# A hybrid attention block: scaling later, another order beside the search, another first attention block

## The chip, the cores and the metric

One core of one Trainium2 chip runs the whole layer in one launch. The metric is the device time of that launch in microseconds, the median of three runs. Most of the text speaks of engines by short names: PE does matmuls (TensorE), DVE is VectorE, ACT is ScalarE, POOL is GpSimd, and SP (SyncE) issues nearly all DMAs, in order.

## The reference

One layer over 2048 tokens of width 1024, in float32:

```python
xn = rms_norm(h, norm_gain)
qa, ka, va, ga, qb, kb, vb, gb, iq, ik, iw, za, zb = split(xn @ w_in)
ya = chunked_relpos_attention(qa, ka, va, rel_bias) * silu(ga)      # 8 heads, own chunk of 64 + 8 before it
yb = dsa_sparse_attention(rope(qb), rope(kb), vb, rope(iq), rope(ik), iw) * silu(gb)
merged = sigmoid(za + b0) * (ya @ w_branch_a) + sigmoid(zb + b1) * (yb @ w_branch_b)
out = rms_norm(h + merged @ w_out, final_norm_gain)
```

The sparse attention scores every admissible key with a small indexer, `score = sum_h relu(iq_h · ik) * iw_h`, keeps the 256 best keys of each query, and attends to those with one shared key and value head.

## The kernel before

**Numbers and tiles.** Every operand of a matmul is split into a high and a low part (names with `h` and `l`, or index 0 and 1), and a product is three matmuls (`mm3`, L210 to L218). ACT makes the high part (a copy to the fast format), DVE or POOL the low part (a subtraction). Tokens come in four groups g of 512. Two slots of transposed, normed x are held on chip (`xh`, `xl`; `SLOT[g]`); groups 0 and 1 use them first, groups 3 and 2 after a reload.

**Units and jobs.** The columns of `w_in` are 20 units: zb and za (four each), gb, ga, qb, va, ka, qa (two each). A standard job is one unit for one group: 2 accumulators of 24 matmuls with 512 columns, or, for the value units va, 4 accumulators of 24 matmuls with 288 columns. Weights come through `wst` (L204 to L209): ACT splits, POOL subtracts.

1. 0 to 100 us: norm, and the projection for the indexer.
2. 100 to 622 us: the first pass, all units for groups 0 and 1. Between its matmuls the indexer's logits are computed (L479 on PE, L481 on ACT, L486 on DVE) and the top-256 threshold of each row is searched: a first guess (L514 to L530), seven passes (L531 to L552, on ACT and DVE in turn), and a sweep (L553 to L569). This work is a set of threads; `tick` pumps them after each accumulator by an amount (`PUMP`, `PUMP2`) against costs that the threads yield. In jobs `EN0` to `EN0 + 15` (8 to 23), `load_early` brings x of groups 3 and 2 and `norm_early` scales it (ACT L1249, POOL L1250), stores it (`xnD`) and forms the block sums that stage 4 uses (`sumD`).
3. 622 to 787 us: the switch. `norm_again` returns queued closures that reload a slot from `xnD`, four for each group, popped from the list `again` during jobs. Then the left-over jobs for groups 3 and 2. When no thread is left, `close_search` adds up whether any row missed its tolerance, which PE does with a 1x1 matmul (L581, tile `bad`); this matmul stands in PE's order.
4. 787 to 1075 us: quads. A unit for groups 2 and 3 and both column halves at once, by Strassen's scheme: 7 products of 12 matmuls, 84 where 96 would stand. `QUADS` lists the 14 units that go so.
5. 1075 to about 1900 us: attention. The list `seq` orders units A(g, h) (a head of branch A for a group) and B(block, heads); `LEAD` units of A come first, then whichever branch is behind by the costs `cost`; `GB` is the order of the groups of B. Each unit's scores run one unit ahead of its outputs, its loads (`qz`, `kk`, `vs`, `qsB`) two ahead. After the last head or block of a group, `extra` places calls of `branch`: 128 columns of `y @ w_branch`, weights through `dst` and `dw`, gate `sig`, result `dt`; the first of the two branches to arrive stores it, the second adds it (`ta`).
6. To 2108 us: output projection (L1457) and the final norm.

**Pools.** Tiles come from pools that are opened at the left or the right end of the on-chip memory. A pool that lies where another lay waits for the last reader there. A tile asked for again in a ring of `bufs` copies waits for the last reader of the copy before.

Of the kernel before, what the change touches and what calls it, by code (L numbers as in the profile page):

```python
# [8 lines left out]
F32 = mybir.dt.float32  # L9
F32R = mybir.dt.float32r  # L10
# [36 lines left out]
WK, WAT = 5, 1  # L47
SPL, LEAD = 96, 3
GB, C0_ = (1, 0, 2, 3), 14
CA_, CB_, TAILB = 26, 9, 260  # L50
# [4 lines left out]
WE = False  # L55
QUADS = "za ka za gb za ka gb zb zb qb ga qa ga qa"
WSB, NB = 4, 5
# [25 lines left out]
def f32(ap):  # L83
    return ap.bitcast(F32)
# [11 lines left out]
def block_kernel(ctx: ExitStack, tc: tile.TileContext, io, dbg=None):  # L96
# [576 lines left out]

    def hl_tile(tag):
        if early_:
            return ev.tile([128, 512], F32R, name=tag + "t", tag="ef")
        return evl.tile([128, 512], F32R, name=tag, tag=tag)

    early_ = []

# [36 lines left out]
    def evac_v(c, g, o, acc):  # L717
        vv = ev.tile([128, 2, 32], F32R, name="vvt", tag="ef") if early_ else evl.tile([128, 2, 32], F32R, name="vv", tag="vv")
        nc.scalar.activation(vv[:, 0], acc[:, 256:288], AF.Copy)
        nc.vector.tensor_tensor(vv[:, 1], acc[:, 256:288], f32(vv[:, 0]), op=OP.subtract)  # L720
        nc.sync.dma_start(vB[:, 4 * g + o, :].rearrange("p (l c d) -> p c l d", l=2, c=2)[:, c], f32(vv))
        acc = acc[:, 0:256]
        e = hl_tile("eh").rearrange("p (h l d) -> p h l d", h=4, l=2)
        v = acc.rearrange("p (h d) -> p h d", h=4)
        nc.scalar.activation(e[:, :, 0, :], v, AF.Copy)
        nc.vector.tensor_tensor(e[:, :, 1, :], v, f32(e[:, :, 0, :]), op=OP.subtract)
        nc.sync.dma_start(vA[g][c * 4:c * 4 + 4, :, o, :].rearrange("h p n -> p h n"), f32(e).rearrange("p h l d -> p h (l d)"))
# [7 lines left out]
    nq = len(quads)  # L735
    rest = [u for k in ("qb", "zb", "za", "gb", "ga", "ka", "qa") for u in left[k]]
    jobs = [("std", u, u, g) for u in range(nu - 2) for g in (0, 1)]
    jobs += [("std", u, u, g) for g in (1, 0) for u in (a_, b_)]
    jobs += [("std", nu + u, u, g) for g in (3, 2) for u in va]
    jobs += [("std", nu + u, u, g) for u in rest for g in (3, 2)]  # L740
    turned = max(i for i, j_ in enumerate(jobs) if j_[3] == 3)
# [40 lines left out]
    def open_early():  # L782

        nonlocal sml, wk, wy, wz, dna, wp_, pe
        dna = dph.enter_context(pool("dna", side="right"))
        wp_ = dph.enter_context(pool("wp_", side="right"))
        sml = ph.enter_context(pool("sml", bufs=4, side="right"))
        wk = ph.enter_context(pool("wk", bufs=2, side="right"))
        wy = ph.enter_context(pool("wy", bufs=2, side="right"))
        wz = ph.enter_context(pool("wz", side="right"))  # L790
        pe = dph.enter_context(pool("pe", space=PSUM, side="right"))

    def open_late():
        nonlocal dn, att, ldb, wp2, pl_ps, psd, kBt, vBt, mk01
        late.append(1)
        dn = dph.enter_context(pool("dn", bufs=2))
        att = ph.enter_context(pool("att"))
# [293 lines left out]
    def branch(m, G, c):  # L1091
# [3 lines left out]
        nc.sync.dma_start(st, io["wA" if m == "a" else "wB"][c])  # L1095
        wt = dn.tile([128, 2, 4, 128], F32R, name="dw", tag="dw", bufs=1)
        nc.scalar.activation(wt[:, 0], st, AF.Copy)  # L1097
# [8 lines left out]
        if (G, c) not in half_done:  # L1106
            half_done.add((G, c))
            nc.sync.dma_start(tD[G, :, c, :], t_)
            return
        ta = dn.tile([128, 512], F32, name="ta", tag="ta")  # L1110
        nc.sync.dma_start(ta, tD[G, :, c, :])
# [61 lines left out]
    def load_m(t):  # L1173

        mts[t] = wp_.tile([128, 2, KT, 256], F32R, name="mm", tag=f"P{(t // 2) % 2}")
        g, o = divmod(t, 4)
        for k in range(0, KT, 2):
            mf = dn.tile([128, 2, 256], F32, name="mf", tag="ta")
            nc.sync.dma_start(mf, mD[g, :, k:k + 2, o * 128:o * 128 + 256])
            nc.scalar.activation(mts[t][:, 0, k:k + 2], mf, AF.Copy)  # L1180
            (nc.vector if t < 2 else nc.gpsimd).tensor_tensor(mts[t][:, 1, k:k + 2], mf, f32(mts[t][:, 0, k:k + 2]), op=OP.subtract)
# [51 lines left out]

    def load_early(g, k):

        xs = tkl.tile([128, 2, 512], F32, name="xs", tag="xs", bufs=2)
        nc.sync.dma_start(xs, io["xT"][g][:, k::4, :])
        xa = None
# [80 lines left out]
    for i, (how, r_, u, g) in enumerate(jobs):  # L1319
        kind, c2 = UNITS[u]  # L1320
        wt, s_ = wcur[r_], SLOT[g]
        rate[0] = PUMP2 if r_ >= nu and kind != "va" else PUMP[2 if i < SLOW else kind in DVE_KINDS]
        if EN0 <= i < EN0 + 16:
            (norm_early if i % 2 else load_early)(3 - (i - EN0) // 8, (i - EN0) // 2 % 4)
        for c in range(4 if kind == "va" else 2):
# [10 lines left out]
            else:  # L1336
# [4 lines left out]
                busy = bool(again) and not early_  # L1341
                for _ in range(1 if busy and len(again) < 3 else 2):
                    if again:
                        again.pop(0)()
# [22 lines left out]
    S2, S1, S4 = (of_sum(n) for n in ("s2", "s1", "s4"))  # L1367
    parts_ = {}

# [192 lines left out]
```

## Time and profile before

| what | value |
|---|---|
| median of 3 runs | 2110.87 us (2108.78 to 2114.64) |
| the profiled execution | 2109.7 us, its span 2107.9 us |
| granted clock of TensorE, mean | 0.986 |
| PE busy | 2006.3 us, 95% |
| DVE, ACT, POOL busy | 70%, 61%, 39% |
| DMA | 333.76 MB, mean 158 GB/s |

The span is the time from the first to the last instruction that the profiler recorded. PE is busy in almost all of it, so the places that matter are the few in which it is not; the windows in the prediction list them. In a row of waits, the numbers are us in total, times, and the longest; in a row of groups, busy us and mean ns, then the idle time ahead of them and what ended it; in a row of the timeline, start and length in us.

### The profile page before, as it was taken

The page shows a single profiled execution, that of the slowest core. Times are in us where ns is not written, and L with a number is a line of the kernel's source. Part 1 is how long each engine was busy: PE and PEld are TensorE (multiplying, and loading weights), DVE is VectorE, ACT ScalarE, POOL GpSimd, SP SyncE. Part 2 cuts the span into 40 slices and gives each one's busy share as a digit, 9 for nine tenths or more (in the row PEclk, how much of TensorE's full clock was granted, in tenths as well). Part 3 has the DMA queues.
Part 4 walks back from the last instruction along what each step waited for, and adds up shares of the span by engine and source line. Part 5 has one row for each costly group of instructions (what it writes and reads, how often), then busy time and mean ns, then how long its engine had stood idle before and what let it go on. Part 6 is the DMA issues. An engine that isn't in the chain of part 4 may idle for free.

```text
span 2107.9 us, 33647 instructions
## 1 busy us (share of the span) xinstructions
PE 2006.3 (95%) x10706; PEld 1693.5 (80%) x10706; DVE 1466.2 (70%) x3738; ACT 1285.3 (61%) x2644; POOL 813.7 (39%) x992
## 2 busy tenths in 40 slices
PE   8798999999998999999979999899999999999998
PEld 7576788889878877878757888788988888888786
DVE  6738888788879667556547676766876678775434
ACT  5465566756565645555449787866987678773221
POOL 2146212231232136545425544566444643434410
PEclk9899999999999999999989999999999999999999
DMA  9487433354564544343564646576345630335642
GB/s 359 145 283 258 151 110 113 110 193 141 171 201 133 176 141 133 109 130 115 165 181 138 191 139 186 174 220 210 111 138 158 187 118 21 101 101 195 203 137 90
DMA packets 225926, 333.76 MB, mean 158 GB/s; under 512 B 28624, under 2 KB 99664, under 8 KB 225616
## 3 DMA queue, kind: packets, MB, share of 16 engines
q1 hardware_dynamic: 225744, 331.57, 49.1%
q8 instruction: 85, 1.39, 0.3%
q14 instruction: 97, 0.79, 0.1%
HBM read 219.33 MB, written 112.16 MB: 157 GB/s over the span
## 4 chain that ended last, share of the span: by engine, by line
PE 62%; DMA 13%; DVE 9%; ACT 5%; POOL 5%; issue 4%; SPq 2%; POOLq 0%; DVEq 0%; ACTq 0%
PE acc L217 23%; PE d L217 6%; PE po L1457 6%; PE O L1053 5%; PE pt L1045 5%; PE s L1028 5%; DMA wst<-wS 4%; PE O L950 3%; PE s L906 2%; PE lg L479 2%; PE pt L940 2%; DMA dst<-wB 1%; PE xa L217 1%; DMA dst<-wA 1%; DVE P L832 1%
## 5 line engine op out<-in xcount | busy, mean ns | idle before, releaser
L217 PE MATMUL acc<-xh,wt 128*128 128x512 f32 x1856 | 605.4, 396 | 5.3 <-DVE e L337 3.3
L217 PEld LDWEIGHTS acc<-xh,wt 128*128 128x128 f32 x1856 | 349.9, 189 | 86.3 <-DVE e L337 3.5
L217 PE MATMUL acc<-xl,wt 128*128 128x512 f32 x928 | 365.9, 394 | 0.0
L209 POOL TENSOR_TENSOR wt<-wst,wt 128x512 fp32r<-128x512 f32 (+1 forms) x108 | 137.6, 1305 | 428.9 <-ACT wt L208 372.3
L853 POOL TENSOR_TENSOR ptl<-pf,pth 128x512 fp32r<-128x512 f32 (+1 forms) x144 | 180.5, 1253 | 227.1 <-ACT pf L849 148.6
L856 DVE TENSOR_TENSOR ptl<-pt,pth 128x512 fp32r<-128x512 f32 (+1 forms) x288 | 187.0, 658 | 46.1 <-ACT pth L855 44.7
L486 DVE SCALAR_TENSOR_TENSOR sc<-lg,iw,sc 128x512 f32<-128x512 f32 (+2 forms) x266 | 179.1, 679 | 52.9 <-ACT lg L481 47.0
L217 PEld LDWEIGHTS acc<-xl,wt 128*128 128x128 f32 x928 | 175.6, 189 | 38.7
L1028 PE MATMUL s<-kBt,qsB 128*128 128x512 f32 (+3 forms) x640 | 184.7, 382 | 2.2 <-DVE mx L832 1.9
L481 ACT ACTIVATE lg<-lg 128x512 f32<-128x512 f32 (+2 forms) x304 | 149.8, 522 | 57.2 <-PE lg L479 55.8
L855 ACT ACTIVATE pth<-pt 128x512 fp32r<-128x512 f32 (+1 forms) x288 | 159.5, 576 | 23.7 <-PE pt L1045 12.7
L1031 ACT ACTIVATE P<-P,mx 128x640 f32<-128x640 f32 (+15 forms) x128 | 154.6, 1209 | 24.0 <-DVE mx L832 23.4
L1045 PE MATMUL pt<-ident,P 128*128 128x128 f32 x1088 | 165.4, 274 | 1.4 <-DVE ptl L856 0.6
L1053 PE MATMUL O<-ptl,vBt 128*128 128x256 f32 x544 | 147.7, 298 | 4.9 <-POOL ptl L853 2.6
L832 DVE CUSTOM_DVE_ANT_0 P<-s,mk,mx 128x512 f32<-128x512 f32 (+2 forms) x192 | 124.9, 651 | 34.5 <-PE s L1028 28.5
L1053 PE MATMUL O<-pth,vBt 128*128 128x256 f32 x544 | 147.0, 289 | 1.3 <-ACT pth L855 0.6
L1045 PEld LDWEIGHTS pt<-ident,P 128*128 128x128 f32 x1088 | 126.3, 140 | 12.0 <-ACT pf L849 1.6
L1098 POOL TENSOR_TENSOR dw<-dst,dw 128x512 fp32r<-128x512 f32 x64 | 82.6, 1291 | 109.4 <-ACT dw L1097 105.5
L906 PE MATMUL s<-kk,qz 128*128 128x256 f32 (+2 forms) x464 | 109.2, 333 | 14.4 <-DMA kk<-kA 9.6
L1028 PEld LDWEIGHTS s<-kBt,qsB 128*128 128x128 f32 x640 | 104.4, 190 | 15.2 <-DVE mx L832 6.4
L217 PE MATMUL acc<-wt,xh 128*128 128x288 f32 x512 | 105.7, 298 | 11.0 <-DVE st L540 8.4
L1053 PEld LDWEIGHTS O<-ptl,vBt 128*128 128x128 f32 x544 | 102.3, 188 | 14.9 <-DVE ptl L856 7.2
(304 smaller groups left out, 4696.7 us busy)
## 6 DMA issues: line engine op xcount, KB each, us to landing
wst<-wP SPq DMA_DIRECT2D x100, 256.0 KB
wst<-wS SPq DMA_DIRECT2D x56, 256.0 KB
kk<-kA SPq DMA_DIRECT2D x56, 256.0 KB
vs<-vA SPq DMA_DIRECT2D x56, 256.0 KB
qz<-qA SPq DMA_DIRECT2D x96, 128.0 KB
xrow<-x SPq DMA_DIRECT2D x16, 512.0 KB
vA<-eh SPq DMA_DIRECT2D x32, 256.0 KB
qsB<-qB SPq DMA_DIRECT2D x16, 512.0 KB
```

The costliest lines, as they stand in the source:

```text
L217: nc.tensor.matmul(acc, a, b, start=(first and i == 0), stop=(last and i == n - 1), **({} if first and last else {"skip_group_check": True}))
L481: nc.scalar.activation(lg, lg, AF.Relu)
L486: nc.vector.scalar_tensor_tensor(o_, lg, wv, o_, op0=OP.mult, op1=OP.add)
L832: nc.vector.tensor_tensor_reduce(dst, ps_, add, 1.0, FMAX if first else mx, OP.add, OP.min, accum_out=mx)
L853: nc.gpsimd.tensor_tensor(lo, pf, f32(hi), op=OP.subtract)
L855: nc.scalar.activation(hi, src, AF.Copy)
L856: nc.vector.tensor_tensor(lo, src, f32(hi), op=OP.subtract)
L906: nc.tensor.matmul(s_ps[:, :w], q[:, m, j * 128:(j + 1) * 128], kk[:, ko:ko + w], start=(m == 0), stop=(m == 1))
L1028: nc.tensor.matmul(s_ps[:, :w], q[:, h, :], kBt[:, m, a:a + w], start=(m == 0), stop=(m == 1))
L1031: nc.scalar.activation(P[:, e, :n], P[:, e, :n], AF.Exp, bias=mx[:, e:e + 1], scale=-1.0, accum_out=sm[:, (u % 2) * 2 + e:(u % 2) * 2 + e ...
L1045: nc.tensor.transpose(pt[:, k, e, :], P[:, e, (kt + k) * 128:(kt + k + 1) * 128], ident)
L1053: nc.tensor.matmul(o_, vBt[:, kt + k, :], src[:, k, :], start=(kt + k == 0 and n_ == 0), stop=(kt + k == b and n_ == 1), skip_group_check= ...
```

## The change

It does five things.

- `load_early` no longer issues its loads as soon as a buffer is free: POOL first copies one element from the low part of the weights of the very job into the tile, so the load of x waits for these weights.
- One more zb unit goes through the quads (15), and `rest`, the order of the left-over units, becomes zb, qb, za; the value units come last. The search is pumped at `PUMP2` through all of these jobs. At a switch of group all reloads that are left are issued at once, and in these jobs two closures are popped after each accumulator.
- `LEAD` is 2 and `GB` (0, 1, 2, 3): block 0 of B is the third unit, and blocks follow in order. The order of units was A00 A01 A02 B4 A03 A04 B4 A05 B5 ..., and is A00 A01 B0 A02 B0 A03 B1 A04 B1 ....
- The branch pool `dn` is opened at the right end, ahead of attention's pools at the left; `dw` has two tiles, `ta` one, and the final stage's `mf` uses the ring of `dt`.
- Evictions between the end of the search and the first quad take tiles from `mid`.

```diff
-SPL, LEAD = 96, 3
-GB, C0_ = (1, 0, 2, 3), 14
+SPL, LEAD = 96, 2
+GB, C0_ = (0, 1, 2, 3), 14
-QUADS = "za ka za gb za ka gb zb zb qb ga qa ga qa"
+QUADS = "za ka za gb za ka gb zb zb zb qb ga qa ga qa"
...
     def hl_tile(tag):
+        if early_ and parts_:
+            return ev.tile([128, 512], F32R, name=tag + "t", tag="ef")
         if early_:
-            return ev.tile([128, 512], F32R, name=tag + "t", tag="ef")
+            return mid.tile([128, 512], F32R, name=tag + "t", tag=f"p{rot('hl', 3)}", bufs=2)
         return evl.tile([128, 512], F32R, name=tag, tag=tag)
...
-        vv = ev.tile([128, 2, 32], F32R, name="vvt", tag="ef") if early_ else evl.tile([128, 2, 32], F32R, name="vv", tag="vv")
+        vv = (mid if early_ else evl).tile([128, 2, 32], F32R, name="vv", tag="vv", bufs=2)
...
-    rest = [u for k in ("qb", "zb", "za", "gb", "ga", "ka", "qa") for u in left[k]]
+    rest = [u for k in ("zb", "qb", "za", "gb", "ga", "ka", "qa") for u in left[k]]
+    rest[1:] = sorted(rest[1:], key=lambda u: UNITS[u][0] != "qb")
...
-    jobs += [("std", nu + u, u, g) for g in (3, 2) for u in va]
-    jobs += [("std", nu + u, u, g) for u in rest for g in (3, 2)]
+    jobs += [("std", nu + u, u, g) for u in rest + va for g in (3, 2)]
...
         dna = dph.enter_context(pool("dna", side="right"))
+        dn = dph.enter_context(pool("dn", bufs=2, side="right"))
...
-        dn = dph.enter_context(pool("dn", bufs=2))
...
-        wt = dn.tile([128, 2, 4, 128], F32R, name="dw", tag="dw", bufs=1)
+        wt = dn.tile([128, 2, 4, 128], F32R, name="dw", tag="dw", bufs=2)
...
-        ta = dn.tile([128, 512], F32, name="ta", tag="ta")
+        ta = dn.tile([128, 512], F32, name="ta", tag="ta", bufs=1)
...
-            mf = dn.tile([128, 2, 256], F32, name="mf", tag="ta")
+            mf = dn.tile([128, 2, 256], F32, name="mf", tag="dt")
...
-    def load_early(g, k):
+    def load_early(g, k, gate):
         xs = tkl.tile([128, 2, 512], F32, name="xs", tag="xs", bufs=2)
+        nc.gpsimd.tensor_copy(xs[:, 0, 0:1], gate)
         nc.sync.dma_start(xs, io["xT"][g][:, k::4, :])
...
-        rate[0] = PUMP2 if r_ >= nu and kind != "va" else PUMP[2 if i < SLOW else kind in DVE_KINDS]
+        if g > 1 and jobs[i - 1][3] != g and not early_:
+            while again:
+                again.pop(0)()
+        rate[0] = PUMP2 if r_ >= nu else PUMP[2 if i < SLOW else kind in DVE_KINDS]
...
-            (norm_early if i % 2 else load_early)(3 - (i - EN0) // 8, (i - EN0) // 2 % 4)
+            at_ = 3 - (i - EN0) // 8, (i - EN0) // 2 % 4
+            if i % 2:
+                norm_early(*at_)
+            else:
+                load_early(*at_, f32(wt[:, 1, KT - 1, 255:256]))
...
-                for _ in range(1 if busy and len(again) < 3 else 2):
+                for _ in range(1 if busy and r_ < nu else 2):
```

What it does to the order of an engine's instructions is shown at three places. First ACT, at the beginning of the first pass (`xs` is the scaling, `lg` the emptying of logits banks, `ef` the eviction of an accumulator). Before:

```order
L693 ACTIVATE ef<-acc,bm 128x512 x3
L208 ACTIVATE wt<-wst 128x4x128
L481 ACTIVATE lg<-lg 128x384
L208 ACTIVATE wt<-wst 128x4x128
L481 ACTIVATE lg<-lg 128x384 x4
L208 ACTIVATE wt<-wst 128x4x128 x2
L1249 ACTIVATE xs<-xs,gcol 128x512 x4
L693 ACTIVATE ef<-acc,bm 128x512
L481 ACTIVATE lg<-lg 128x384 x3
```

Now, at the first scaling:

```order
L534 ACTIVATE jk_1794,sm<-sc,st 128x640
L695 ACTIVATE ef<-acc,bm 128x512
L481 ACTIVATE lg<-lg 128x384 x2
L1252 ACTIVATE xs<-xs,gcol 128x512 x2
L481 ACTIVATE lg<-lg 128x512 x2
L695 ACTIVATE ef<-acc,bm 128x512
L481 ACTIVATE lg<-lg 128x512 x2
L481 ACTIVATE lg<-lg 128x384
```

Before, the first four scalings stood behind the third eviction; now two of them stand behind the thirteenth, and the rest follow in pairs.

Second, PE around the closing matmul of the search (L581). Before:

```order
L217 MATMUL acc<-xl_125,wt 128x512
L217 MATMUL acc<-xh_124,wt 128x512 x2
L217 MATMUL acc<-xl_125,wt 128x512
L217 MATMUL acc<-xh_124,wt 128x512
L581 MATMUL lg<-ones,bad 1x1
L217 MATMUL acc<-xh_122,wt 128x512
L217 MATMUL acc<-xl_123,wt 128x512
```

Now:

```order
L217 MATMUL acc<-wt,xh_124 128x288 x2
L217 MATMUL acc<-wt,xl_125 128x288
L217 MATMUL acc<-wt,xh_124 128x288 x2
L217 MATMUL acc<-wt,xl_125 128x288
L581 MATMUL lg<-ones,bad 1x1
L217 MATMUL acc<-wt,xh_118 128x288 x2
L217 MATMUL acc<-wt,xl_119 128x288
```

Between the last logits matmul (L479) and this row stand 209 matmuls with 512 columns before, and 157 with 288 columns now: value units surround it in place of standard ones.

Third, SP from the last stores of q to the loads of the third unit of A (`qz`, `kk`); `kBt`, `vBt`, `bres`, `qsB`, `mk`, `sgB` are loads for branch B. Before:

```order
L996 DMA qsB<-qB_73 128x8x128
L1004 DMA mk<-mskD 128x640
L996 DMA qsB<-qB_73 128x8x128
L715 DMA qA_62<-eht 128x512
L715 DMA qA_62<-part 128x512
L1004 DMA mk<-mskD 128x768
L1188 DMA kBt<-kB 64x2x512 x2
L1190 DMA vBt<-vB 128x512
L1188 DMA kBt<-kB 64x2x512 x2
L1190 DMA vBt<-vB 128x512
L865 DMA qz_12102<-qA_60 64x512 x3
L869 DMA kk<-kA_64 128x512
```

Now:

```order
L1192 DMA vBt<-vB 128x512
L717 DMA qA_63<-eht 128x512
L717 DMA qA_63<-part 128x512
L885 DMA sg<-gAD_82 128x512
L717 DMA qA_62<-eht 128x512
L717 DMA qA_62<-part 128x512
L998 DMA qsB<-qB_72 128x8x128 x2
L1006 DMA mk<-mskD 128x384
L1001 DMA sgB<-gBD_86 128x4x128
L1006 DMA mk<-mskD 128x512
L867 DMA qz_12162<-qA_60 64x512 x3
L871 DMA kk<-kA_64 128x512
```

The last of the key and value loads (`vBt`) now stands ahead of the last two pairs of q stores where all of them stood behind, and the small loads for the block that is now third stand between those stores and `qz`.

More of the change, by code (lines that the diff above doesn't have):

```diff
@@ L674, in hl_tile @@
     def hl_tile(tag):
+        if early_ and parts_:
+            return ev.tile([128, 512], F32R, name=tag + "t", tag="ef")
         if early_:
-            return ev.tile([128, 512], F32R, name=tag + "t", tag="ef")
+            return mid.tile([128, 512], F32R, name=tag + "t", tag=f"p{rot('hl', 3)}", bufs=2)
         return evl.tile([128, 512], F32R, name=tag, tag=tag)
-    early_ = []
+    early_, parts_ = [], {}
     def evac(kind, ct, g, acc, own=None):
@@ L782, in open_early @@
     def open_early():
-        nonlocal sml, wk, wy, wz, dna, wp_, pe
+        nonlocal sml, wk, wy, wz, dna, dn, wp_, pe
         dna = dph.enter_context(pool("dna", side="right"))
+        dn = dph.enter_context(pool("dn", bufs=2, side="right"))
         wp_ = dph.enter_context(pool("wp_", side="right"))
@@ L793, in open_late @@
     def open_late():
-        nonlocal dn, att, ldb, wp2, pl_ps, psd, kBt, vBt, mk01
+        nonlocal att, ldb, wp2, pl_ps, psd, kBt, vBt, mk01
         late.append(1)
-        dn = dph.enter_context(pool("dn", bufs=2))
         att = ph.enter_context(pool("att"))
@@ L1367, in block_kernel @@
     S2, S1, S4 = (of_sum(n) for n in ("s2", "s1", "s4"))
-    parts_ = {}
     def product(acc, w, x_, first, last):
```

## The prediction

> **What bounds the kernel now.** I read the page's head first, then the time windows, since a share over the span mixes stages.
>
> ```profile
> span 2107.9 us, 33647 instructions
> PE 2006.3 (95%) x10706; PEld 1693.5 (80%) x10706; DVE 1466.2 (70%) x3738; ACT 1285.3 (61%) x2644; POOL 813.7 (39%) x992
> ```
>
> TensorE is the bound: 2107.9 − 2006.3 = 101.6 us of idle PE is all that moving work can win. The windows say where that idle time lies (from:to, length, then busy us and count of PE, weight loads, DVE, ACT, POOL; granted clock; DMA share; GB/s).
>
> ```profile
> 0.00:100.00 100.00, 77.02 (x388) 64.17 (x388) 67.80 (x145) 50.73 (x103) 21.53 (x119) 0.93 0.70 251
> 100.00:250.00 150.00, 138.41 (x587) 108.27 (x588) 98.36 (x256) 85.54 (x178) 70.75 (x56) 0.99 0.71 236
> 250.00:600.00 350.00, 350.00 (x1698) 295.08 (x1698) 293.25 (x704) 211.78 (x407) 71.87 (x55) 1.00 0.44 143
> 600.00:650.00 50.00, 38.98 (x201) 33.67 (x200) 46.60 (x108) 31.96 (x55) 22.11 (x18) 0.93 0.63 206
> 650.00:787.00 137.00, 135.01 (x700) 116.15 (x699) 100.91 (x240) 69.33 (x125) 29.16 (x28) 0.99 0.43 140
> 787.00:1075.00 288.00, 279.22 (x1185) 222.49 (x1184) 170.62 (x377) 144.62 (x369) 144.50 (x288) 0.99 0.41 133
> 1075.00:1100.00 25.00, 12.92 (x62) 11.11 (x61) 8.26 (x37) 10.48 (x29) 5.67 (x9) 0.73 0.96 244
> 1100.00:1300.00 200.00, 194.38 (x1264) 169.47 (x1263) 151.16 (x459) 170.49 (x396) 99.39 (x103) 1.00 0.53 160
> 1300.00:1350.00 50.00, 43.41 (x250) 36.55 (x249) 30.86 (x92) 33.21 (x79) 22.29 (x26) 0.97 0.65 193
> 1350.00:1900.00 550.00, 538.29 (x3515) 476.04 (x3515) 404.78 (x1068) 427.28 (x796) 265.97 (x245) 1.00 0.44 136
> ```
>
> PE idles 23.0 us in the first 100 (not touched), 11.6 in 100–250 (where the early scaling lies), none in 250–600, 11.0 at the switch to groups 3 and 2, 2.0 up to the end of the search, 8.8 in the quads, 12.1 + 5.6 as attention starts, 6.6 in 1300–1350 (the first cluster of branches), 11.7 up to 1900. The change works at five of these places.
>
> **The change part by part.** The profiled execution took 2109.7 us (span 2107.9 and 1.8 around it), 1.2 below the median of 2110.87; the sum goes by 2109.7.
>
> *Early scaling.* Waits in 100–250, the POOL scaling there, and one small DVE operation of the search with POOL busy (120–210) and not (250–450):
>
> ```profile
> PE lg L479 <- DVE sc L486: 10.5, 9, 2.2
> ACT xs L1249 <- DMA xs<-xT: 13.7, 5, 5.4
> L1250 POOL TENSOR_TENSOR xs<-xs,roots 128x512 f32<-128x512 f32 x16 | 20.2, 1288 | 14.4 <-ACT xs L1249 14.4
> L545 DVE COPY_PREDICATED st<-msk,st 128x8 f32<-128x8 int32 x7 | 3.9, 553 | 0.2
> L545 DVE COPY_PREDICATED st<-msk,st 128x8 f32<-128x8 int32 x18 | 3.0, 169 | 0.5
> ```
>
> PE waits 10.5 us for logits banks that DVE frees late; ACT, which empties the banks before DVE, stands 13.7 us in its own queue behind loads of xT. The change puts the scaling some ten accumulators later and gates each load, so both causes leave this window; eight gate copies on POOL are hidden beside its 70.75 us in 150. The most to win is the window's 11.6. Against it: 32 POOL operations of about 1.29 us (41 us) come into a stretch with 71.87 POOL and 293.25 DVE us in 350. The seven L545 of the first of these rows lost (553 − 169) × 7 = 2.7 us of DVE; if six of the search's small operations lost as much, some 17 us went to the 43 or so POOL operations there, 0.4 each, and the 32 moved ones bring DVE 13 us. DVE has 350 − 293 = 57 free, so most of that is absorbed: bounds −11.6 and +4, and I take **−8**, nearer the gain because PE had no idle time at all in 250–600.
>
> The Trainium skill ("SBUF — State Buffer", section "Who interferes with whom") calls the port pair of DVE and GpSimd an exclusive lock held for a whole instruction. By it one moved POOL operation could hold a DVE operation for its full 1.29 us, and the estimate is 41 us of DVE and not 13; the L545 rows agree with the kind of loss and show a third of that size. What the full size would give is the third rival below.
>
> *Order at the switch.* Waits of PE in 600–650; then, from the timeline, the first matmul after the first pass and the last reload of slot 0 on DVE:
>
> ```profile
> PE acc L217 <- DVE st L540: 8.4, 1, 8.4
> PE acc L217 <- DVE el L712: 2.5, 1, 2.5
> 622.46 0.42 PE L217 MATMUL acc<-wt,xh 128*128 128x288 f32 x2
> ...
> 641.62 0.69 DVE L1264 TENSOR_TENSOR xl<-xl,xh 128x512 fp32r<-128x512 f32 x1
> ```
>
> Both waits (10.9) are accumulators of the value units, 3.2 us of PE each, whose eviction queues behind search passes on DVE, busy 46.60 of 50. zb's accumulators last 5.6 us and are evicted by ACT alone, so these waits go. In their place slot 0 must be reloaded after one job (48 matmuls × 0.2325 = 11.2 us) and not two value jobs. PE leaves the first pass at 622.46 and would want the fourth block of slot 0 nine matmuls into the next job, at 622.46 + 11.2 + 2.1 = 635.8; the row has it at 642.3. Bounds of the new wait 0 and 6.5; I take 4, since the reloads are now issued at once. Net **−7** (−10.9 to −4.4).
>
> *Tail of the search.* Last logits matmul, seven matmuls for the rate, the closing matmul that waits for `bad`, the search pass on ACT, and the forms in 650–700, where PE never idled:
>
> ```profile
> 719.69 0.40 PE L479 MATMUL lg<-ikT,iqT 128*128 128x512 f32 x1
> 719.92 0.39 PE L217 MATMUL acc<-xl,wt 128*128 128x512 f32 x1
> ...
> 721.55 0.63 PE L217 MATMUL acc<-xh,wt 128*128 128x512 f32 x2
> 770.52 0.19 PE L581 MATMUL lg<-ones,bad 128*1 128x1 f32 x2 [1.99 <-DVE bad L578]
> L534 ACT ACTIVATE jk<-sc,st 128x2048 int8<-128x2048 f32 x7 | 14.0, 2003 | 7.2 <-DVE st L552 5.7 <-DVE st L529 1.5
> L217 PE MATMUL acc<-wt,xh 128*128 128x288 f32 x192 | 38.6, 295 | 0.0
> L217 PE MATMUL acc<-wt,xl 128*128 128x288 f32 x96 | 28.2, 294 | 0.0
> L479 PE MATMUL lg<-ikT,iqT 128*128 128x512 f32 x25 | 8.1, 394 | 0.0
> L217 PE MATMUL acc<-xh,wt 128*128 128x512 f32 x18 | 5.9, 393 | 0.0
> L217 PE MATMUL acc<-xl,wt 128*128 128x512 f32 x9 | 3.5, 394 | 0.0
> ```
>
> (721.55 − 719.92) / 7 = 0.2325 us a matmul of 512 columns; (50 − 52 × 0.2325) / 288 = 0.132 for one of 288. From the last logits to `bad` it is 770.52 − 719.69 = 50.8 us, seven dependent passes that need ACT (2.0 each) and then DVE, and a final sweep. Some 3 us are lost behind POOL and other ACT work, so 47.8 is the least. PE covers that now with 209 matmuls of 512 columns (48.6 us), and waits 1.99. In the changed order 157 matmuls of 288 columns stand there: 20.7 us. PE then waits 47.8 − 20.7 = 27.1 to 30.1. Less the 2.0 of today: **+25** (to +28), the largest term, and the one against the change.
>
> *After the search.* Eight accumulators of value work (192 matmuls × 0.132 = 25 us) stand between the closing matmul and the first quad, where 72 × 0.2325 = 16.7 us stood. PE's waits in 787–800:
>
> ```profile
> PE acc L217 <- DVE wv L1317: 2.1, 1, 2.1
> PE acc L217 <- ACT wv L1316: 1.9, 1, 1.9
> PE acc L217 <- ACT wt L1316: 1.0, 1, 1.0
> ```
>
> These 5.0 us wait for weights and sums of the first quad, whose loads start when the search closes; with 8 us more cover I take **−4** (−5 to −2). *One quad more*: 12 fewer matmuls (96 become 84) × 0.2325 = **−2.8**; its weights' splitting lies beside quads in which DVE, ACT and POOL have half their time free (288 us: 170.62, 144.62, 144.50); without that cover a quad's wait is of the kind above, 1 to 2 us.
>
> *Start of attention.* The stall, two of SP's issues before it, and the first windows after:
>
> ```profile
> 1083.44 0.32 SPq L1190 DMA_DIRECT2D vBt<-vB  x1
> 1087.67 0.58 SPq L869 DMA_DIRECT2D kk<-kA  x1
> 1094.50 0.66 PE L906 MATMUL s<-kk,qz 128*128 128x128 f32 x2 [9.56 <-DMA kk<-kA]
> 1100.00:1130.00 30.00, 27.73 (x178) 22.59 (x176) 24.94 (x88) 28.26 (x74) 15.57 (x18) 1.00 0.50 150
> ```
>
> kk for the third unit is issued 4.2 us after vBt and lands 6.8 us later, while PE stands still for 9.56. In the new order the key and value loads stand ahead of the last q stores, and the third unit is a pair of heads of block 0, which needs no kk; A02's kk is wanted one unit (some 4 us) later. Of 9.56 + 2.5 I take **−8** (bounds −10 and +5: with light units of attention A beside light blocks 0 to 2, ACT, 28.26 of 30 here, may set the pace; the second rival).
>
> *Branches.* Waits of PE in 1300–1350, and of POOL on ACT over the span:
>
> ```profile
> PE d L217 <- ACT dw L1097: 4.5, 2, 3.0
> L1098 POOL TENSOR_TENSOR dw<-dst,dw 128x512 fp32r<-128x512 f32 x64 | 82.6, 1291 | 109.4 <-ACT dw L1097 105.5
> ```
>
> A second `dw` lets ACT and POOL split the next weights while PE reads these, but the staging tile is still single, and there are now two clusters of 16 where there was one. Bounds −6.6 (all of the window) and +5 (a second window like it); **−3**. With `ta` single and `mf` on the ring of `dt`, the output projection is taken at 0: PE is at 198.65 of 208 behind 1900, and these loads run ahead.
>
> Sum: −8 − 7 + 25 − 4 − 2.8 − 8 − 3 = −7.8, so 2109.7 − 7.8 = **2102 us**.
>
> **The rivals.**
>
> *Slower: the tail of the search is dearer than its own chain.* If DVE reaches the last logits with work still queued (it was 46.60 of 50 busy at the switch, and the pump now runs at its high rate through the value units), every microsecond of backlog adds to the 27. With 7 us of backlog, 3 lost behind POOL, the whole 6.5 at slot 0 and no gain after the search: −7.8 + 7 + 3 + 2.5 + 4 = +8.7, about 2119. For it speaks that evictions of value units need DVE too; against it that DVE had 100.91 of 137 us in 650–787. It decides once the wait at the closing matmul passes 35 us.
>
> *ACT sets the pace of the first attention units.* Then the cheap blocks leave PE idle while ACT works, as at 1100–1130 but for longer: +5 in place of −8, 2115. For it: ACT's 94% in that row; against: the same ACT work must be done in either order, and 9.56 us of it now waits for a load.
>
> *The scaling slows the search where it lands.* If each moved POOL operation holds DVE for 1.29 us, 41 of DVE's 57 free us go, the waits for banks come back later in the pass: 0 or +4 in place of −8, 2110 to 2114.
>
> *The gains hold and the search ends early enough.* If the windows with PE idle at the start of attention (17.7 us) and at the branches (18.3) are halved by loads that run ahead, −18 in place of −11, and early scaling and switch give all (−22.5 in place of −15): 2109.7 + 25 − 6.8 − 18 − 22.5 = 2087.
>
> **How the numbers follow.** The sum as it stands (2096 to 2108) has 0.38, the dear tail 0.20, the ACT pace 0.12, the slowed search 0.12, the full gains 0.18. About 0.3% (6.3 us) is what a measurement of this kernel can tell from no change. Of the first case two thirds lie below 2104.5; with the last that makes faster 0.45. Slower than 2117 is most of the dear tail and a part of the next two, 0.27; 0.28 is left between. The terms' own bounds reach from 2088 (gains whole, tail +25) to beyond 2130; leaving out a tenth on each side gives 2086 to 2122. The likeliest case alone has 2096 to 2108.
>
> **What would show it.** Right: no wait of logits for DVE before 200 us; the closing matmul idle for 25 to 30 us with `bad` as releaser; a wait of zero to 7 us at the second job of the switch; no kk stall over 3 us near 1090. Wrong: a closing matmul that hardly waits (then more work covers it than I counted and the time is near 2080), or PE idle in 250–600, or a first 100 us of attention longer than now.

## The result

The changed kernel is slower: 2129.64 us, the median of 5 runs (2124.28 to 2133.16), against 2111.02 for the kernel before on the same chip; ratio 1.0078, 95% interval [1.0054, 1.0102]. The forecast was 2102 us, with a range of 2086 to 2122. The profiled execution took 2125.1 us with a span of 2123.3, 15.4 above the span before (the medians differ by 18.6).

The head of its page and its windows, in the same stretches (length, then busy us and count of PE, weight loads, DVE, ACT, POOL; clock; DMA share; GB/s):

```profile
span 2123.3 us, 33669 instructions
PE 2007.7 (95%) x10694; PEld 1691.9 (80%) x10694; DVE 1484.8 (70%) x3763; ACT 1287.3 (61%) x2661; POOL 820.4 (39%) x1016
...
100.00:250.00 150.00, 148.11 (x647) 120.49 (x648) 106.95 (x317) 88.89 (x183) 38.76 (x33) 0.99 0.54 173
250.00:600.00 350.00, 342.51 (x1645) 285.14 (x1644) 293.96 (x642) 208.87 (x402) 107.82 (x86) 1.00 0.52 171
600.00:650.00 50.00, 45.76 (x185) 35.96 (x184) 47.86 (x104) 35.46 (x54) 20.81 (x16) 0.93 0.57 190
650.00:787.00 137.00, 107.50 (x618) 96.18 (x617) 103.89 (x248) 66.62 (x127) 35.64 (x41) 0.90 0.41 135
787.00:1075.00 288.00, 285.27 (x1227) 228.85 (x1226) 170.00 (x391) 145.74 (x383) 146.91 (x292) 1.00 0.41 132
1100.00:1300.00 200.00, 183.75 (x1132) 157.39 (x1133) 134.95 (x414) 150.18 (x370) 105.98 (x111) 0.99 0.62 188
```

PE's idle time fell by 9.7 us in 100–250 and rose by 7.5 in 250–600. It fell by 6.8 in 600–650 and rose by 27.5 in 650–787. In 1100–1300 it rose by 10.6. The waits behind this, from the lists of PE's waits in 250–400, 600–790 and 1075–1130:

```profile
PE lg L479 <- DVE sc L486: 7.0, 8, 2.3
...
PE lg L581 <- DVE bad L578: 28.6, 1, 28.6
PE acc L217 <- DVE xl L1267: 3.9, 1, 3.9
...
PE s L908 <- DMA kk<-kA: 2.4, 1, 2.4
```

Windows at fixed times mix in the shift of what came before. So I also read from PE's timeline when each stage begins: the first matmul behind the first pass, the first scores of attention (`s<-kk`), the first matmul of the output projection (`po`).

| stretch | before, us | after, us | difference | forecast |
|---|---|---|---|---|
| start to the end of the first pass | 622.5 | 621.0 | −1.5 | −8 |
| switch, search, quads | 452.9 | 465.9 | +13.0 | +11.2 |
| attention with its branches | 813.8 | 818.0 | +4.2 | −11 |
| output projection | 218.7 | 218.4 | −0.3 | 0 |
| span | 2107.9 | 2123.3 | +15.4 | −7.8 |

The second row came nearly as worked out. The first and the third did not, and they miss by 6.5 and 15.2 us.

One trace is one execution, and stages differ between executions. Nine kernels of this document, that of before among them, have the same program up to the end of the first pass; their traces end it at 618.9 to 624.7 us. Six have the attention of before, and take 813.3 to 819.6 us for it. Differences of that size between two traces prove nothing by themselves.

The experiments begin by taking the change apart.

### The profile page after: what moved, and what is told of

It reads as the page before. It is cut to its first block, busy times and chain, and to the rows that moved or that the text cites. A ratio compares the mean times of both kernels' runs of the same rounds, so it can differ in the third digit from the quotient of the medians.

```text
span 2123.3 us, 33669 instructions
## 1 busy us (share of the span) xinstructions
PE 2007.7 (95%) x10694; PEld 1691.9 (80%) x10694; DVE 1484.8 (70%) x3763; ACT 1287.3 (61%) x2661; POOL 820.4 (39%) x1016
## 4 chain that ended last, share of the span: by engine, by line
PE 36%; DMA 9%; POOL 6%; ACT 5%; DVE 4%; issue 3%; SPq 0%; POOLq 0%; DVEq 0%; ACTq 0%
PE po L1466 8%; PE d L217 5%; PE O L1055 5%; DMA wst<-wS 4%; PE pt L1047 4%; PE s L1030 4%; PE O L952 3%; PE s L908 2%; PE acc L217 2%; DMA dst<-wA 2%; PE pt L942 2%; DMA dst<-wB 1%; DVE P L834 1%; POOL wst L1315 1%; ACT P L1033 1%
## 5 line engine op out<-in xcount | busy, mean ns | idle before, releaser
L217 PE MATMUL acc<-xh,wt 128*128 128x512 f32 x1824 | 595.8, 396 | 3.2 <-DVE e L337 2.2
L217 PEld LDWEIGHTS acc<-xh,wt 128*128 128x128 f32 x1824 | 344.0, 189 | 81.3 <-DVE e L337 2.5
L217 PE MATMUL acc<-xl,wt 128*128 128x512 f32 x912 | 360.2, 395 | 4.2 <-DVE xl L1267 3.9
L209 POOL TENSOR_TENSOR wt<-wst,wt 128x512 fp32r<-128x512 f32 (+1 forms) x104 | 137.0, 1348 | 293.9 <-ACT wt L208 244.9
L857 ACT ACTIVATE pth<-pt 128x512 fp32r<-128x512 f32 (+1 forms) x288 | 159.5, 580 | 17.8 <-PE pt L1047 6.8
L1033 ACT ACTIVATE P<-P,mx 128x128 f32<-128x128 f32 (+15 forms) x128 | 154.3, 1207 | 15.3 <-DVE mx L834 14.8
L534 ACT ACTIVATE jk<-sc,st 128x640 int8<-128x640 f32 (+6 forms) x49 | 71.2, 1453 | 75.6 <-DVE st L552 63.5
L479 PE MATMUL lg<-ikT,iqT 128*128 128x512 f32 (+2 forms) x304 | 106.3, 374 | 9.4 <-DVE sc L486 7.0
```

What stands on the lines that cost most here:

```text
L217: nc.tensor.matmul(acc, a, b, start=(first and i == 0), stop=(last and i == n - 1), **({} if first and last else {"skip_group_check": True}))
L857: nc.scalar.activation(hi, src, AF.Copy)
L1033: nc.scalar.activation(P[:, e, :n], P[:, e, :n], AF.Exp, bias=mx[:, e:e + 1], scale=-1.0, accum_out=sm[:, (u % 2) * 2 + e:(u % 2) * 2 + e ...
```

## The experiments

Ratios are against the kernel before, run on the same chip in the same set of runs.

| kernel | ratio | 95% interval |
|---|---|---|
| early scaling alone | 1.0010 | 1.0000 to 1.0020 |
| jobs and the fifteenth quad | 1.0096 | 1.0079 to 1.0113 |
| order of attention's units alone | 0.9970 | 0.9961 to 0.9980 |
| branch pool, whole | 1.0049 | 1.0033 to 1.0065 |
| fifteenth quad alone | 1.0078 | 1.0057 to 1.0099 |
| order of jobs, 14 quads | 1.0090 | 1.0073 to 1.0107 |
| branch pool to the right, old tiles | 0.9973 | 0.9963 to 0.9983 |
| the same, with one `ta` | 0.9957 | 0.9941 to 0.9974 |
| order of units and pool right | 0.9929 | 0.9909 to 0.9949 |
| changed kernel, closing matmul held | 1.0032 | 1.0016 to 1.0048 |
| changed kernel, one `dw` | 0.9986 | 0.9976 to 0.9996 |
| last version | 0.9887 | 0.9864 to 0.9909 |

### The four parts, one at a time

Early scaling alone. The edit is the gate of `load_early`:

```diff
+        nc.gpsimd.tensor_copy(xs[:, 0, 0:1], gate)
         nc.sync.dma_start(xs, io["xT"][g][:, k::4, :])
```

> The kernel before with one part of the change: the loads of x for groups 3 and 2 wait for the weights of their own job. Theory A (the waits move with the scaling): PE's 10.5 us of waits for logits banks leave 100-250 and come back between 200 and 400, where the scaling now runs, about 7 us of them; net -1 to -3 us, about 2108 to 2110. Theory B (the prediction: DVE has room there): -8 us, 2103, and no such wait behind 250.

Jobs: `QUADS` with the third zb, `rest + va`, `PUMP2` for all, and the tiles from `mid`.

> The kernel before with only the order of the left-over jobs, the fifteenth quad and what they need. Theory A (the uncovered tail of the search is the whole loss): the closing matmul waits 27 to 30 us for bad, the switch loses its 11 us of waits, and the time is 11 to 14 us above the kernel before. Theory B (the tail is covered by something else and the loss is in attention): within 4 us of before.

Order of attention's units:

```diff
-SPL, LEAD = 96, 3
-GB, C0_ = (1, 0, 2, 3), 14
+SPL, LEAD = 96, 2
+GB, C0_ = (0, 1, 2, 3), 14
```

> The kernel before with only LEAD 2 and blocks in the order 0, 1, 2, 3. Theory A (the order of the units sets PE's idle time in attention: light blocks pair with light heads, and a cluster of 16 branches comes late): 4 to 8 us slower than before. Theory B (the order is harmless and what attention lost comes from the moved branch pool): -3 to +1 us. In either the stall for kk at the start of attention is shorter than 9.56 us, since the third unit needs no kk.

Branch pool: `dn` opened in `open_early` at the right, `dw` twice, `ta` once, `mf` in the ring of `dt`.

> The kernel before with only the branch pool at the right end, two dw tiles, one ta tile and mf in the ring of dt. Theory A (order of the units costs): the key and value loads start earlier, the kk stall shrinks from 9.56 to 3 us or less, 5 to 8 us faster than before. Theory B (the pool costs): 2 to 5 us slower, with PE's waits in the branches or at the start of the output projection.

Early scaling gains nothing. Theory A's waits came back (8.0 us in 200–400), but its net gain of 1 to 3 us did not show (+2, interval 0 to 4). The jobs cost even more than the 11 to 14 us expected (+20), with the wait of 28.6 us for `bad` that theory A named. The order of units gains 6 us where theory A expected a loss and B nothing to speak of. The pool costs 10 (theory B, at twice its size). So the ACT pace that I had feared for the light units is not there, and the pool, which I had priced at a gain, is one of the two losses. The four do not add: 0.1 + 0.96 − 0.30 + 0.49 = 1.25%, where the whole change has 0.78%; why was not followed further.

### Quad or order of jobs

```diff
-QUADS = "za ka za gb za ka gb zb zb qb ga qa ga qa"
+QUADS = "za ka za gb za ka gb zb zb zb qb ga qa ga qa"
```

> The kernel before with only the fifteenth quad (a zb unit more); value units stay first after the switch. 197 matmuls of 512 columns (45.8 us) then stand between the last logits and the closing matmul. Theory A (the order of the jobs makes the loss, not the quad): the closing matmul waits 2 to 5 us, the time is 0 to 3 us below before. Theory B (the quad takes the cover away): the closing matmul waits 15 us or more and the time is 8 us or more above before.

The other half is the change of jobs without this line:

> The kernel before with the new order of the left-over jobs (value units last) but its 14 quads. 64 matmuls of 512 and 72 of 288 columns (24.4 us) stand between the last logits and the closing matmul. Theory A (the fifteenth quad alone makes the loss, by taking standard work away from beside the search): 0 to 5 us below before. Theory B (the place of the closing matmul among the jobs makes a loss of its own): it waits 23 to 28 us, nothing waits at the first quad, and the time is 7 to 13 us above before; the two losses do not add in the changed kernel, since both are the same search that ends too late.

Each half alone costs nearly the whole: +0.78% and +0.90%, together +0.96%. Theory B holds in both, but not in every size: the quad's wait for `bad` is 8.6 us and not 15 or more, and the new order costs 19 us where 7 to 13 were expected. From the switch to the end of the quads, where both work, their traces lose 10.2 and some 14 us; the rest of the ratios lies elsewhere. PE's waits in 700–790 and 790–850 with the fifteenth quad alone, then in 600–1075 with the new order alone:

```profile
PE lg L581 <- DVE bad L578: 8.6, 1, 8.6
...
PE acc L217 <- ACT wv L1316: 12.1, 2, 11.2
```

```profile
PE lg L581 <- DVE bad L578: 23.7, 1, 23.7
PE acc L217 <- DVE eht L728: 4.9, 2, 4.7
PE acc L217 <- DVE xl L1266: 4.4, 1, 4.4
```

With the quad, 22.3 us of standard work (96 matmuls × 0.2325) leave the time in which the search runs, and their replacement waits behind the search, because quads need its memory and load after it. PE then waits 8.6 us for the search, and 12.1 for the first quad's weights. With the new order, the work is there but stands behind the closing matmul in PE's order. That suggests one search that ends too late for PE, met in two ways.

Holding the closing matmul tests that:

```diff
-        elif not early_:
+        elif not early_ and not hold[0]:
             close_search()
...
+        hold[0] = i < len(jobs) - 1
```

> The changed kernel, with the closing matmul of the search (and the opening of the pools behind it) held until the last job of standard work: 325 matmuls of 288 columns and 13 of 512 (46 us) then cover the search's tail where 20.7 us did. Theory A (the uncovered tail is the loss): the wait for bad falls from 28.6 to 2 to 6 us; about 5 us of it come back as waits of the first quad for weights and sums that are loaded later; 12 to 20 us below the changed kernel, 2107 to 2117. Theory B (the wait at the closing matmul only stands in for another one, such as the loads of the first quad): within 5 us of the changed kernel.

PE's waits in 700–790:

```profile
PE lg L581 <- DVE bad L578: 12.9, 1, 12.9
PE acc L217 <- ACT part L1390: 7.0, 1, 7.0
```

The ratio falls from 1.0078 to 1.0032, some 10 us. The wait fell from 28.6 to 12.9, not to 2 to 6: by PE's timeline the time from the last logits to the closing matmul grew from 49.9 to 60.2 us. The evictions of value units run on DVE, and more of them now stand between the search's passes; that they are the cause of the growth was not tested. And 7.0 us came back at the first quad, with 2.6 more in 790–850 where the changed kernel waits 0.4: more than the 5 expected. So the result lies between the two theories. By the traces, the stage from the switch to the end of the quads shrinks only from 465.9 to some 461.6 us; attention, which the edit does not touch, from 818.0 to 812.4. The uncovered tail is a part of the loss, and this test does not show that it is all of it.

### Branch pool: the place or the tiles

> The kernel before with only the branch pool at the right end; dw single, ta double and mf in its ring as before. Theory A (the tiles cost, two dw and one ta, not the place): the stall for kk goes (9.56 to 3 us or less) and nothing is lost in the branches: 4 to 7 us faster than before. Theory B (the place costs): as slow as with the whole change of the pool, 8 to 12 us above before.

> The branch pool at the right end, with one ta tile and mf in the ring of dt, but a single dw. Right end alone was 0.9973 of before, with all of the pool's change 1.0049. Theory A (two dw tiles cost: ACT takes up the split of the next weights earlier and stands in its queue for their load): 0.997 to 0.999 of before, ACT's waits for dst as before (about 46 us). Theory B (the single ta costs, a load of ta behind each addition on POOL): 1.003 to 1.006, with POOL's waits for ta of about 15 us as with the whole change.

Right end alone is 0.9973, with the single `ta` 0.9957, with the second `dw` as well 1.0049. The place and the single `ta` cost nothing (theory A of both, though the wait for kk fell to 5.8 us and not to 3, and the second ratio is a little below its range). So the second `dw` costs 0.9%, some 19 us, by itself: in attention alone, 825.5 us against 807.9 in the traces. ACT's waits for `dst`, and DVE's for ACT, in 1075–1900, with two `dw`:

```profile
ACT dw L1097 <- DMA dst<-wB: 41.7, 15, 6.6
ACT dw L1097 <- DMA dst<-wA: 33.5, 16, 5.2
...
DVE ptl L856 <- ACT pth L855: 67.3, 59, 4.8
```

and with one:

```profile
ACT dw L1097 <- PE d L217: 18.8, 12, 4.3
ACT dw L1097 <- DMA dst<-wB: 18.0, 8, 4.2
ACT dw L1097 <- DMA dst<-wA: 15.0, 6, 4.2
...
DVE ptl L856 <- ACT pth L855: 50.9, 65, 4.2
```

ACT's waits for the load are 75.2 us with two and 33.0 with one (39.4 before). The one load that PE waits for there is kk, 5.6 and 5.9 us, so it is not the loads for attention that come later. One of ACT's waits on its timeline, with two `dw`, and what PE did meanwhile:

```profile
1421.69 0.18 ACT L910 ACTIVATION_READ_ACCUMULATOR P<-P,mx 128x1 f32 x1
1428.49 0.63 ACT L1097 ACTIVATE dw<-dst 128x512 fp32r<-128x512 f32 x1 [6.61 <-DMA dst<-wB]
1429.03 0.58 ACT L855 ACTIVATE pth<-pt 128x512 fp32r<-128x512 f32 x1
1429.51 0.59 ACT L848 ACTIVATE pth<-pt 128x512 fp32r<-128x512 f32 x1
1429.98 0.60 ACT L849 ACTIVATE pf<-pt 128x512 f32<-128x512 f32 x1
```

```profile
1429.66 0.50 PE L950 MATMUL O<-pth,vs 128*128 128x512 f32 x1 [2.43 <-ACT pth L855]
```

ACT stands still for 6.61 us at the split of branch weights that are not there yet. Behind it in its queue are three conversions of attention probabilities, which PE and DVE need. PE had written their inputs (`pt`) by 1422.4, so they wait for their place in the queue alone. With one `dw`, the split's place in ACT's order is later, since it must follow the branch before; the single `dst` is loaded meanwhile. With two, the split has moved ahead of the load.

To test this, the loads were left out (the weights of one branch serve all 64, so the result is another one), with two `dw` and with one:

```diff
-        nc.sync.dma_start(st, io["wA" if m == "a" else "wB"][c])
+        if not held:
+            held.append(dn.tile([128, 4, 128], F32, name="dst", tag="dst", bufs=1))
...
+        st = held[0]
```

Both kernels also stage the weights of the output projection in the tiles of `sig` and `dt` in place of `dst`; this is the same in the two, so they are to be held against each other.

> The branch pool's whole change (two dw tiles), with the branch weights loaded once and used for all 64 branches; 63 loads of 256 KB are left out, so the merged result is not the reference's. To be held against the next kernel, the same with one dw tile. Theory A (ACT stands in its queue behind the loads of dst, which two dw tiles let it reach earlier): the two kernels are within 3 us of each other, and ACT's waits for dst (75 us between 1075 and 1900 with the loads) are gone. Theory B (the second tile costs by itself, by the splits standing ahead of attention's own work on ACT): this kernel stays 12 us or more above the next.

> The control for the kernel above: branch pool at the right, one ta tile, one dw tile, the branch weights loaded once (63 loads left out). Theory A: about as fast as the one above, and 3 to 8 us below the same kernel with its loads (0.9957 of before). Theory B: 12 us or more below the one above.

Without loads, two `dw` have 0.9971 [0.9958, 0.9985] and one has 0.9939 [0.9915, 0.9963]: a difference of 0.32% where it was 0.92% with loads. ACT's waits for `dst` are gone (0.9 and 0.8 us). So about two thirds of the loss goes with the loads, by the ratios. In attention alone, the traces differ by 3.1 us (804.2 and 801.1) where they differed by 17.6 with the loads. The difference that is left, 6.7 us by the ratios, lies between what the two theories expected, and the two intervals overlap a little; whether the second tile costs 0.3% in another way is not settled.

Does it hold within the whole change?

```diff
-        wt = dn.tile([128, 2, 4, 128], F32R, name="dw", tag="dw", bufs=2)
+        wt = dn.tile([128, 2, 4, 128], F32R, name="dw", tag="dw", bufs=1)
```

> The changed kernel with one dw tile in place of two, nothing else. Theory A (the second tile is the loss behind 1075): 15 to 20 us below the changed kernel, about 2110 to 2115, so no slower than before by more than 0.2%, with the 28 us wait at the closing matmul still in it. Theory B (that loss belongs to the pool's change on the old order of units only): within 5 us of the changed kernel.

It does: 0.9986 in place of 1.0078. The stretch of attention falls from 818.0 to 800.3 us, by 17.7, while the wait for `bad` stays at 28.6. ACT's waits for `dst` in 1075–1900, of the changed kernel and then with one `dw`:

```profile
ACT dw L1099 <- DMA dst<-wA: 32.6, 15, 4.8
ACT dw L1099 <- DMA dst<-wB: 31.8, 13, 5.0
```

```profile
ACT dw L1099 <- DMA dst<-wA: 11.1, 10, 2.5
ACT dw L1099 <- DMA dst<-wB: 8.5, 3, 5.3
```

### Why the early scaling gained nothing

> The kernel with the gated early scaling alone, with POOL's part of the scaling and of the block sums left out (32 operations; loads, stores and ACT's part stay; so groups 3 and 2 are not normed by their row factor). Theory A (POOL's operations slow the small operations of the search on DVE): the 7 us of PE's waits for logits banks behind 200 us fall to 2 or less, and L545's operation returns from about 0.49 to 0.17 us; 5 to 8 us below the gated kernel. Theory B (ACT standing in its queue behind the loads of x delays the logits): 5 us or more of these waits stay.

The edit leaves out the five `tensor_tensor` calls of `norm_early`. Ratio 0.9933 [0.9914, 0.9953] from two executions, against 1.0010 with them. PE's waits for logits in 100–600, gated with POOL's part, then without it (where 250–600 has none):

```profile
PE lg L479 <- DVE sc L486: 4.9, 5, 2.5
PE lg L479 <- DVE sc L484: 3.5, 2, 3.3
```

```profile
...
PE lg L479 <- DVE sc L484: 0.7, 1, 0.7
```

One of the search's small operations in the groups of 180–400, with POOL's part, then without:

```profile
L548 DVE TENSOR_TENSOR sm<-sm,st 128x2 f32<-128x2 f32 x20 | 6.3, 314 | 0.5
```

```profile
L548 DVE TENSOR_TENSOR sm<-sm,st 128x2 f32<-128x2 f32 x22 | 3.5, 158 | 0.5
```

The waits go when POOL's work goes, while ACT still waits for the loads of x in 180–400 (17.8 us, 24.6 with POOL's part). So at this place it is POOL, and ACT standing in its queue is at most the smaller part: theory A. What POOL costs where the scaling stood before was not tested. The gain by the ratios, some 16 us, is twice what was expected. The two traces differ by 13.9 us: 6.6 are PE's idle time in 100–600, 3.0 lie in the first 100 us, which the edit does not touch, and the rest was not traced to a cause.

The Trainium skill ("SBUF — State Buffer", section "Who interferes with whom") says that a DVE instruction with two inputs in on-chip memory contends with POOL, and one with a single input, outside the fast modes, does not. In the changed kernel's 250–400 the trace agrees for two inputs (L548). Of two operations with one input, L549 agrees and L544 does not:

```profile
L548 DVE TENSOR_TENSOR sm<-sm,st 128x2 f32<-128x2 f32 x11 | 4.8, 440 | 0.2
...
L544 DVE TENSOR_SCALAR st<-st 128x4 f32<-128x4 f32 x10 | 4.3, 426 | 0.0
...
L549 DVE TENSOR_SCALAR sm<-sm 128x2 f32<-128x2 f32 x11 | 1.8, 159 | 0.0
```

Before, the means in this window were 157 ns for L548, 165 for L544 and 160 for L549. Whether L544 ran in a fast mode no run shows. In the last version below L549 is slowed too (221 ns in 180–400), so what a single input saves is not settled.

The prediction read from a mean of 553 ns that such an operation loses a third of POOL's 1.29 us. The mean hides what happens: most operations lose nothing, and a few stand until the POOL operation ends. One such place, DVE and then POOL:

```profile
320.89 1.31 DVE L547 TENSOR_TENSOR sm<-st 128x4 f32<-128x4 f32 x1
322.24 1.22 DVE L548 TENSOR_TENSOR sm<-sm,st 128x2 f32<-128x2 f32 x1
323.38 0.16 DVE L549 TENSOR_SCALAR sm<-sm 128x2 f32<-128x2 f32 x1
323.49 1.22 DVE L544 TENSOR_SCALAR st<-st 128x4 f32<-128x4 f32 x1
```

```profile
320.89 2.56 POOL L1253 TENSOR_TENSOR xs<-xs,roots 128x512 f32<-128x512 f32 x2 [6.97 <-ACT xs L1252]
323.39 1.30 POOL L1258 TENSOR_TENSOR xa<-xs,xa 128x512 f32<-128x512 f32 x1
```

Of the 108 small operations of the search (L541 to L552) in 250–400, 18 took more than 0.3 us, and each of these ended within 0.05 us of the end of a POOL operation. Seven of the 18 stood beside the splitting of weights (L209), which the change does not move.

### Versions that gain

> The kernel before with LEAD 2, blocks in order, and the branch pool at the right end with its old tiles. If the place of the pool and the order of units are gains that add: 8 to 13 us below before. If both took away the same stall for kk, the pool adds nothing to the order: 5 to 7 us below before.

The two gains add: 0.9929, where their product is 0.9943. That is 15 us, more than the 8 to 13 expected. The wait for kk falls from 9.6 to 3.0 us, and PE's idle time in 1175–1375 from 8.0 to 3.0; what the rest comes from was not looked for.

> The kernel before with what gained (LEAD 2, blocks in order, branch pool at the right with its old tiles), plus value units last with 14 quads and the closing matmul held to the second job from the end, so that 53 us of matmuls stand in the search's tail. If covering the tail frees the switch's gain (no 11 us of waits at the switch, a wait for bad of 10 us or less): 0 to 6 us below the same kernel with the old job order, 2086 to 2093. If the search then ends later, because the evictions of value units share DVE with it: equal or up to 6 us above it, 2092 to 2099.

The ratio is 0.9918 [0.9902, 0.9935]. In 600–1075 PE waited 1.5 us for `bad` and 3.9 at slot 0, but 7.8 for the first quad's weights (`ACT wv`). Against 0.9929 this is no difference that the intervals can tell. But with more work in the tail the new order no longer loses: the stage from the switch to the end of the quads takes some 450 us, where before it took 452.9. The last version adds the single `ta` (with `mf` in the ring of `dt`), and the gated scaling with DVE in place of POOL:

```diff
-        e = nc.gpsimd
+        e = nc.vector
```

> The best kernel so far (order of units, branch pool right, value units last with 14 quads and the closing matmul held; 0.9918 of before) with one ta tile and the gated early scaling, whose 32 POOL operations run on DVE. Without them the gated kernel ran 14 us below its like. Theory A (POOL's operations cost by holding DVE's small ones): 22 us of DVE work replaces about 13 us of held DVE time and POOL's long operations, and DVE has 57 us free in the pass: 3 to 10 us below the best so far. Theory B (any further 20 us on DVE delay the search as much): within 3 us of it.

2083.72 us, ratio 0.9887 [0.9864, 0.9909], 25 us below the kernel before and the fastest of all (theory A: 6 us below the version before). Its early scaling on DVE, and its waits for logits in 250–600:

```profile
L1253 DVE TENSOR_TENSOR xs<-xs,roots 128x512 f32<-128x512 f32 x16 | 10.9, 687 | 6.7 <-ACT xs L1252 6.6
```

```profile
PE lg L479 <- DVE sc L486: 2.3, 4, 0.8
```

An operation takes 687 ns on DVE where POOL took 1288 and slowed DVE besides. The interval of this version and that of the one before overlap a little, and two edits lie between them. The traces tell them apart: the first pass ends at some 612 us in place of 624, and attention takes 799.9 in place of 797.4. So the step from 0.9918 lies where the scaling is. The four kernels with the gated scaling on POOL end the first pass at 618.0 to 621.0.

## Why the prediction was wrong

Two steps failed: that DVE's idle time absorbs what POOL costs it, and that a second `dw` saves time because weights are split earlier.

*Early scaling, −8: wrong.* Measured −1.5 in the trace and +0.10% alone. The waits left 100–250 as forecast and came back between 250 and 400 (7.0 us), which the prediction had named as a sign of being wrong. The size of what DVE loses was about right: 13 us were estimated; L548 lost (440 − 157) × 11 = 3.1 us in 250–400, and five operations of its kind (L545, L547, L548, L551, L552) together some 13. It was not 0.4 us for every POOL operation, though, but whole holds of a few. The step that failed is "DVE has 350 − 293 = 57 free, so most of that is absorbed". A logits bank waits for one eviction at one time; a late DVE delays it even where DVE idles elsewhere. That PE had not waited in 250–600 before was no reserve, only the absence of the cause. The third rival had the mechanism, and 0.12 of the chance; its 41 us for DVE were three times too many.

*Switch, −7: right.* The waits of value units went (0.3 us left), and slot 0 cost 3.9 where 4 was taken.

*Tail of the search, +25: right.* 28.6 us of wait, within 27.1 to 30.1; the time from the last logits to the closing matmul is 49.9 us where 47.8 to 50.8 were taken. *After the search, −4: right.* In 790–850 PE waited 0.4 us in all.

*One quad more, −2.8: wrong by itself.* It was costed as 12 matmuls fewer, with the splitting hidden. Alone it makes the kernel 0.78% slower, about 16 us, and 10.2 in its own stage by the traces. What it removes is 22.3 us of work from the only place where work was short; that cover was reckoned, but under the order of jobs alone. In the sum this did not show, since the 25 us of tail held the loss of both: beside the new order the kernel has 1.0096 with the quad and 1.0090 without, which the intervals do not tell apart.

*Start of attention, −8: right.* The kk wait fell from 9.56 to 2.4 us. The order of units gains 0.30% alone, the pool at the right 0.27%.

*Branches, −3: wrong, and the largest miss.* "A second `dw` lets ACT and POOL split the next weights while PE reads these, but the staging tile is still single": the second half of that sentence was the answer, taken as a limit on the gain. The term was −3 with a bound of +5. With one `dw` in place of two the changed kernel is 0.92% faster, some 19 us, of which 17.7 lie in attention: the split moves ahead of its load on ACT, and ACT waits 64.4 us for `dst` in place of 19.6. What stood behind the waiting instruction on ACT, the conversions for attention, was not asked.

The rivals: the dear tail did not come (28.6 us of wait, not over 35), nor ACT's pace. So the kernel was slower by a path that none of the rivals had, next to the tail that the sum had already.

## What to carry to other kernels

A second buffer behind a single one can move the waiting to an earlier place in an engine's queue, as it did here on ACT; look at what stands behind it there, not only at what the buffer frees. Work that is to run beside a long dependent chain is worth its cover, and taking it away to save matmuls can cost more than they do (here some 16 us for 2.8). Idle time of an engine over a stretch is no reserve for a wait that depends on when it gets to one instruction.

## What was not expected of the hardware

POOL's operations of 1.29 us made small operations of DVE stand until they ended: in the changed kernel's 250–400, 18 of 108 took more than 0.3 and up to 1.31 us where the others took some 0.16, and the mean of one with two inputs (L548) rose from 157 to 440 ns. DVE had idle time over the whole stretch, and PE still waited 7.0 us for logits there. Leaving 32 such POOL operations out took all of PE's waits for logits in 250–600 away; moving them to DVE, at 687 ns each, left 2.3 us.
